# Attention probabilities turned by VectorE in 32x32 squares and a round trip through DRAM, in place of TensorE transposes

## The chip, the cores and the metric

One core of one Trainium2 chip runs the whole program in a single launch. The metric is the device time of one execution in microseconds (us). Of the kernel before, three runs gave a median of 2538.5 us.

## What is computed

A trunk of two layers works on one sequence of 1024 tokens with 1024 features in f32. Layer 0 mixes tokens with a gated MLP and a gated delta rule; layer 1 with differential attention; both have an MLP and a gated projection behind the mixing. The change touches only the attention of layer 1, whose core is:

```python
for each of 8 heads, each block of 128 queries:
    logits = einsum('qrd,krd->rqk', q_blk, k) - slope * dist      # r = 0, 1: two maps, 64 features each
    logits = where(dist >= 0, logits, -inf)
    probs = softmax(logits, axis=-1)
    attn = probs[0] - lam * probs[1]                              # (128 queries, keys)
    o = einsum('qk,ke->qe', attn, v)                              # e = 128 value features
o = rms_norm(o, sub_gain) * (1 - lam_init)
```

The product with the values sums over keys. TensorE sums over the partition, so `attn`, which is made with queries on the partitions, has to be turned to have keys there.

## The kernel before

**Work of the stage.** `attention` (L872) runs 64 blocks, eight for each of eight heads; block b of a head has 128 queries and the n = 128(b+1) keys up to its own. A block makes its two maps of logits on TensorE (`logits`, L1002); VectorE takes them out of PSUM with the position term and keeps a running minimum (L1016); ScalarE takes the exponential with the sum (L1019). `combine` (L1021) forms map 0 plus a factor times map 1 on VectorE, over n columns, in place in map 0. `transpose` (L1029) turns each 128x128 square on TensorE into a PSUM tile `pt` of four squares (L1035), and ScalarE copies that to an SBUF tile `aT` (L1037). `value` (L1039) multiplies by the values, one product for each block of keys (L1046), and takes the result out (L1047, L1049); after each fourth block o is scaled on GpSimd and stored (L1065). Map 0 has three buffers that take turns (`lg0`), map 1 has one (`lg1`), and `aT` three (`aT_tag`, L953).

**Work between.** While a head attends, the projections of the heads to come run in between: q and k of the next head, and half of a set of values for two heads (`proj_qk`, `proj_v`, L908 and L932), 24 units for a head. Their weights come by SP's queue into eight raw buffers (L101), are split into a high part on ScalarE (L223) and a low part on GpSimd (L224), and each unit is 12 products of 256 columns. In the last head there are no projections left; parts of the output projection take their place, which load and store h (`mix_part`, L1165).

**Order.** The main loop (L1133) is written as a pipeline. In turn g it emits: logits of map 0 of block g, `combine` of block g-1, a share of the projections, `transpose` of block g-2, a share, logits of map 1 of block g, a share, `value` of block g-2, a share. This is a priority and not the final order: when the program is built, a planner lays out each engine's instructions by estimated times, so that later work may be put ahead of earlier work that isn't ready. On the chip each engine then takes its own list strictly in order, SP's list of transfers too.

**Values.** A tile of values (`A0`, `A1`) holds two heads' 256 features for all tokens, tile t of 128 tokens with one token on each partition. ScalarE writes it from PSUM in L938, and the products of L1046 read it.

Of the kernel before, what the change touches and what calls it, by code (L numbers as in the profile page):

```python
# [11 lines left out]
F32 = mybir.dt.float32  # L12
F32R = mybir.dt.float32r
AF = mybir.ActivationFunctionType
ALU = mybir.AluOpType
# [3 lines left out]
P = 128  # L19
# [3 lines left out]
NT = S // P  # L23
HT = 512
# [90 lines left out]
class Trunk:  # L115
# [731 lines left out]
    def attn_consts(self, q_gain, k_gain, lam, sub_gain, lam_init):  # L847
# [21 lines left out]
        nc.vector.tensor_scalar(nl, nl, -lam_init, None, ALU.add)  # L869
        self.qg, self.kg, self.sg, self.nlam = qg, kg, sg, nl  # L870

    def attention(self, w_qkv, w_out, gain_next, h_dram):  # L872

        nc = self.nc
        NB = NT
        hs, r = list(self.hs), list(self.r)
# [16 lines left out]
        def proj(label, srcs, t2s, evac):  # L893
            def units(w):
                for t2 in t2s:
                    ps = self.mm_ps()
                    for i in range(2):
                        h, c = tok(2 * t2 + i)
                        for k in range(KT):
                            self.mm3(ps[:, 256 * i : 256 * (i + 1)], [x[:, c] for x in hs[h][k]], w.at(k), k == 0, k == KT - 1)  # L900
                            if k == 3 or (k == 7 and i == 0):
                                yield None
                    yield evac(t2, ps)

            n = 256 // len(srcs)
            return Proj(label, [(ap, i * n) for i, ap in enumerate(srcs)], 256, units, 4 * len(t2s), nc.gpsimd)

        def proj_qk(hd, qk):  # L908
# [20 lines left out]

            return proj(f"qk{hd}", [w_qkv[:, i * D + hd * P : i * D + (hd + 1) * P] for i in range(2)], range(4), evac)  # L930

        def proj_v(pr, hf, out):  # L932
            def evac(t2, ps):
                if len(out) == pr:
                    out.append(self.slot(f"A{pr % 2}", [P, NT, 256], F32, "v"))
                for i in range(2):
                    t = 2 * t2 + i
                    nc.scalar.activation(out[pr][:, t, :], ps[:, 256 * i : 256 * (i + 1)], AF.Copy, scale=r[t // 4][:, t % 4 : t % 4 + 1])  # L938

            return proj(f"v{pr}", [w_qkv[:, 2 * D + pr * 256 : 2 * D + (pr + 1) * 256]], (2 * hf, 2 * hf + 1), evac)  # L940

# [8 lines left out]
        lg0 = [lgs[0][:, 0], lgs[0][:, 1], lgs[1][:, 0]]  # L950
        lg1 = lgs[1][:, 1]
        qk_tag = itertools.cycle(("aux", "sc", "aux"))
        aT_tag = itertools.cycle(("c8", "c9", "c10"))  # L953
        heads = {}

        def begin(hd):

            qk = qks[hd]

            ks = self.slot(f"A{2 + hd % 2}", [P, 2, S], F32R, "ks")  # L960

            def put_k(hf):
                pt = self.aux([P, HT], "tr", "tr")
                for t in range(4):
                    self.pe.transpose(pt[:, t * P : (t + 1) * P], qk[1][hf][:, t, :], self.ident)
                for r in range(2):
                    own, other = half[r], half[1 - r]
                    dst = ks[:, r, hf * HT : (hf + 1) * HT]
                    nc.scalar.activation(dst[own], pt[own], AF.Copy, scale=self.kg[own])
                    nc.vector.scalar_tensor_tensor(dst[other], pt[own], self.kg[own], f32(dst[own]), ALU.mult, ALU.subtract)  # L970

            def put_q(b2):
                pt = self.aux([P, HT], "tr", "tr")
                for i in range(2):
                    self.pe.transpose(pt[:, i * P : (i + 1) * P], qk[0][b2 // 2][:, 2 * (b2 % 2) + i, :], self.ident)
                qh = self.slot(f"c{11 + b2 % 2}", [P, 2, 2 * P], F32R, "qh")
                ql = qlow[b2 % 2]
                for r in range(2):
                    own, other = half[r], half[1 - r]
                    nc.scalar.activation(qh[own, r], pt[own, 0 : 2 * P], AF.Copy, scale=self.qg[own])  # L980
                    nc.vector.tensor_copy(qh[other, r], f32(qh[own, r]))
                    nc.vector.scalar_tensor_tensor(ql[own, r], pt[own, 0 : 2 * P], self.qg[own], f32(qh[own, r]), ALU.mult, ALU.subtract)
                return qh, ql

            put_k(0)
            heads[hd] = [ks, put_k, put_q, put_q(0)]

        class Block:
# [32 lines left out]
            def combine(me):  # L1021
                b, n, sums = me.b, me.n, me.sums

                rs = self.sp.tile([P, 1], F32, tag="rs", name=self.nm("rs"))
                nc.vector.reciprocal(rs, sums[:, b, 1:2])
                nc.vector.scalar_tensor_tensor(rs, sums[:, b, 0:1], self.nlam, rs, ALU.mult, ALU.mult)
                nc.vector.scalar_tensor_tensor(me.lg[0][:, :n], me.lg[1][:, :n], rs, me.lg[0][:, :n], ALU.mult, ALU.add)

            def transpose(me):  # L1029
                me.aT = []  # L1030
                for c in range((me.n + HT - 1) // HT):
                    k0, k1 = 4 * c, min(me.b + 1, 4 * c + 4)
                    pt = self.aux([P, HT], "tr", "tr")
                    for k in range(k0, k1):
                        self.pe.transpose(pt[:, (k - k0) * P : (k - k0 + 1) * P], me.lg[0][:, k * P : (k + 1) * P], self.ident)  # L1035
                    me.aT.append(self.slot(next(aT_tag), [P, HT], F32, "aT"))
                    nc.scalar.copy(me.aT[c][:, : (k1 - k0) * P], pt[:, : (k1 - k0) * P])  # L1037

            def value(me):  # L1039
                hd, b = me.hd, me.b  # L1040
# [53 lines left out]
        qks, vs, os = [[] for _ in range(8)], [], [[] for _ in range(8)]  # L1094

        projs = [proj_v(0, 0, vs), proj_qk(0, qks[0]), proj_v(0, 1, vs)]
        for hd in range(1, 8):
            projs.append(proj_qk(hd, qks[hd]))
            if hd < 7:
                projs.append(proj_v((hd + 1) // 2, (hd + 1) % 2, vs))  # L1100
# [8 lines left out]
        def pump():  # L1109
            i = state[0] = state[0] + 1  # L1110
            for (i0, u0), (i1, u1) in zip(marks, marks[1:]):
                if i0 < i <= i1:
                    want = u0 + (u1 - u0) * (i - i0) / (i1 - i0)
                    while state[1] < want:
                        next(fill)
                        state[1] += 1
            if i > TAIL:
                next(tail, None)
# [13 lines left out]
        blocks = []  # L1132
        for g in range(8 * NB + 2):  # L1133
            if g < 8 * NB:
                hd, b = divmod(g, NB)
                blocks.append(Block(hd, b))
                blocks[g].logits(0)
            if 0 < g <= 8 * NB:
                blocks[g - 1].combine()
            pump()  # L1140
            if g < 8 * NB and b % 2 and b < NB - 1:
                q = heads[hd][2]((b + 1) // 2)
            if g > 1:
                blocks[g - 2].transpose()
            pump()
            if g < 8 * NB:
                if b == 3 - (hd < 7):
                    heads[hd][1](1)
                blocks[g].logits(1)
            pump()  # L1150
            if g > 1:
                blocks[g - 2].value()
            pump()
            if g < 8 * NB:
                if b % 2 and b < NB - 1:
                    heads[hd][3] = q
                if b == 6 + (hd == 6) and hd < 7:
                    begin(hd + 1)
# [824 lines left out]
```

## Time and profile before

| | |
|---|---|
| median of three runs | 2538.5 us (2537.97 to 2539.23) |
| the profiled execution: its span, first to last instruction | 2535.2 us |
| median less span | 3.3 us |
| TensorE, matmul records | 2515.3 us, 99% of the span |
| VectorE | 1854.3 us, 73% |
| ScalarE | 1285.9 us, 51% |
| GpSimd | 285.5 us, 11% |
| DMA of the core | 396.92 MB in 298,818 packets, mean 157 GB/s |

The profile gives no time of the profiled execution other than its span, from the first to the last instruction. PE is TensorE's multiplication, PEld its loading of weights, which runs beside it; DVE is VectorE, ACT ScalarE, POOL GpSimd, SP the engine that issues the transfers. A busy time is the union of an engine's records. Durations of single matmuls overlap, since they are pipelined, so the spacing of a row of them says more than the length of one. The granted TensorE clock was full nearly throughout (mean 0.999).

### The profile page before, as it was taken

The numbers are of one execution on the slowest core, as the hardware profiler recorded it, in microseconds if no ns is written. First come the engines' busy times: TensorE is split into PE (matmuls) and PEld (weight loads), VectorE is DVE, ScalarE is ACT, GpSimd is POOL, SyncE is SP. The second block draws the span as 40 slices with busy tenths as digits, with TensorE's granted clock in tenths as the row PEclk, the third lists the DMA queues.
The fourth block names the chain that finished last, engine by engine and source line by source line (L and its number), as shares of the span: only waits on it lengthen the run. The fifth ranks groups of instructions, "written<-read, shape, count | busy, mean of one in ns | idle before, by whom it ended". The sixth has DMA issues, their size and how long they took to land.

```text
span 2535.2 us, 40147 instructions
## 1 busy us (share of the span) xinstructions
PE 2515.3 (99%) x14046; PEld 2151.9 (85%) x14046; DVE 1854.3 (73%) x3676; ACT 1285.9 (51%) x2553; POOL 285.5 (11%) x256
## 2 busy tenths in 40 slices
PE   9999999999999999999999999999999999999999
PEld 7898898888888878888999999988778888888877
DVE  7867776697666888656477777787887677787586
ACT  6543444465455434544366666665654555445452
POOL 0301232000000000000334333310000000000000
PEclk9999999999999999999999999999999999999999
DMA  7452435457557756553211111147466558655651
GB/s 242 126 157 78 136 110 193 138 175 242 161 174 257 245 164 207 183 158 120 74 53 47 55 47 43 59 136 257 143 219 202 174 184 281 216 184 185 200 178 59
DMA packets 298818, 396.92 MB, mean 157 GB/s; under 512 B 37780, under 2 KB 165752, under 8 KB 298616
## 3 DMA queue, kind: packets, MB, share of 16 engines
q1 hardware_dynamic: 298600, 394.36, 48.4%
q8 instruction: 110, 1.80, 0.3%
q14 instruction: 92, 0.75, 0.1%
q10 hardware_dynamic: 16, 0.00, 0.0%
HBM read 289.40 MB, written 104.86 MB: 156 GB/s over the span
## 4 chain that ended last, share of the span: by engine, by line
PE 92%; DVE 4%; DMA 2%; issue 1%; ACT 1%; SPq 0%; POOL 0%; DVEq 0%; ACTq 0%; POOLq 0%
PE mm L76 79%; PE po L76 3%; PE qk L76 2%; PE aux L76 2%; PE tr L79 2%; DMA raw<-in_w_ple_gate_dram 1%; DVE lg L1016 0%; DVE w L224 0%; DMA raw<-in_w_mlp_dram 0%; PE pz L76 0%; PE py L76 0%; PE aux L79 0%; PE pvn L76 0%; PE pab L79 0%; PE pkq L76 0%
## 5 line engine op out<-in xcount | busy, mean ns | idle before, releaser
L76 PE MATMUL mm<-g,w 128*128 128x512 f32 x2592 | 603.6, 394 | 0.8 <-DVE g L224 0.5
L223 ACT CAST w<-raw 128x512 fp32r<-128x512 f32 x598 | 366.0, 618 | 453.8 <-PE mm L76 386.8
L76 PEld LDWEIGHTS mm<-g,w 128*128 128x128 f32 x2592 | 485.9, 188 | 116.2 <-DVE g L224 1.0
L76 PE MATMUL mm<-hi,w 128*128 128x512 f32 x1728 | 553.6, 396 | 0.3 <-ACT hi L1219 0.3
L76 PE MATMUL mm<-w,hi 128*128 128x256 f32 (+2 forms) x2528 | 505.5, 295 | 0.0
L224 DVE TENSOR_TENSOR w<-raw,w 128x512 fp32r<-128x512 f32 x534 | 364.8, 690 | 178.9 <-ACT w L223 169.4
L76 PEld LDWEIGHTS mm<-w,hi 128*128 128x128 f32 x2528 | 400.1, 188 | 13.6 <-DVE acc L284 0.3
L76 PEld LDWEIGHTS mm<-hi,w 128*128 128x128 f32 x1728 | 324.7, 188 | 73.7 <-ACT hi L1219 0.7
L76 PE MATMUL mm<-w,lo 128*128 128x256 f32 (+2 forms) x1264 | 370.3, 293 | 0.0
L76 PE MATMUL mm<-lo,w 128*128 128x512 f32 x864 | 341.6, 396 | 0.9 <-DVE lo L1220 0.9
L76 PE MATMUL mm<-t,w 128*128 128x512 f32 x1152 | 270.9, 394 | 1.2 <-ACT w L223 1.2
L76 PEld LDWEIGHTS mm<-t,w 128*128 128x128 f32 x1152 | 216.2, 188 | 52.8 <-ACT w L223 1.6
L76 PEld LDWEIGHTS mm<-w,lo 128*128 128x128 f32 x1264 | 238.2, 188 | 5.6
L76 PEld LDWEIGHTS mm<-lo,w 128*128 128x128 f32 x864 | 162.8, 188 | 36.8 <-DVE lo L1220 1.4
L224 DVE TENSOR_TENSOR g<-graw,g 128x512 fp32r<-128x512 f32 x216 | 147.2, 685 | 8.8 <-DMA gd<-g 6.9
L223 ACT CAST g<-graw 128x512 fp32r<-128x512 f32 x216 | 132.7, 617 | 32.8 <-issue 10.9
L1019 ACT ACTIVATE lg<-lg,nm 128x128 f32<-128x128 f32 (+7 forms) x128 | 99.5, 777 | 82.5 <-DVE nm L1016 76.0
L260 POOL TENSOR_TENSOR r<-ms,mhalf 128x4 f32<-128x4 f32 x12 | 13.3, 1109 | 1060.9 <-DVE ms L258 1033.5
L350 ACT ACTIVATE g<-g 128x512 f32<-128x512 f32 x96 | 60.6, 632 | 114.8 <-DVE g L284 114.5
L1016 DVE CUSTOM_DVE_ANT_0 lg<-qk,al 128x512 f32<-128x512 f32 (+3 forms) x128 | 75.1, 589 | 36.2 <-PE qk L76 32.8
L224 POOL TENSOR_TENSOR w<-raw,w 128x512 fp32r<-128x512 f32 x64 | 84.6, 1347 | 111.9 <-ACT w L223 63.0
L76 PE MATMUL mm<-ohi,w 128*128 128x512 f32 x256 | 85.2, 400 | 0.5 <-ACT ohi L1073 0.5
(336 smaller groups left out, 3612.4 us busy)
## 6 DMA issues: line engine op xcount, KB each, us to landing
raw<-in_w_mlp_dram SPq DMA_DIRECT2D x352, 256.0 KB, 3.3
graw<-gd SPq DMA_DIRECT2D x224, 256.0 KB, 2.8
gd<-g SPq DMA_DIRECT2D x192, 256.0 KB, 3.1
raw<-in_w_ple_gate_dram SPq DMA_DIRECT2D x76, 256.0 KB, 3.5
acc<-h_dram SPq DMA_DIRECT2D x64, 256.0 KB, 4.4
keep<-in_w_mlp_dram SPq DMA_DIRECT2D x64, 256.0 KB, 4.3
raw<-in_w_in_e_dram SPq DMA_DIRECT2D x60, 256.0 KB, 3.7
h_dram<-acc SPq DMA_DIRECT2D x48, 256.0 KB, 2.5
```

The lines of the kernel that those rows point to most:

```text
L76: self._next(self.engine.matmul(*a, **k))
L79: self._next(self.engine.transpose(*a, **k))
L223: self.nc.scalar.copy(hi, src)
L224: (lo_engine or self.nc.vector).tensor_tensor(lo, src, f32(hi), ALU.subtract)
L260: nc.gpsimd.tensor_tensor(r, ms, self.mhalf[:, 0:4], ALU.pow)
L350: nc.scalar.activation(g, src, AF.Relu)
L1016: nc.vector.tensor_tensor_reduce(out=lg[:, k0:k1], in0=ps[:, : k1 - k0], in1=al[:, u0 + k0 : u0 + k1], scale=-1.0, scalar=3.0e38 if c == 0 ...
L1019: nc.scalar.activation(lg[:, :n], lg[:, :n], AF.Exp, bias=nm[:, r, nch - 1 : nch], scale=-1.0, accum_out=me.sums[:, b, r : r + 1])
```

## The change

The turning of `attn` leaves TensorE and ScalarE. `combine` writes into map 1's buffer, and VectorE turns every 32x32 square of it in place of the square, into map 0's buffer. What then lies in partition 32i+c, column 32j+r of a block of keys is query 32i+r and key 32j+c. One transfer stores the block's rows to a new DRAM tile in pieces of 512 B; one transfer for each four blocks of keys loads them back in pieces of 128 B, so that partition 4c+j holds key 32j+c, and its columns are the 128 queries in order. That is a complete turn, but for the order of keys in the partitions. The sum over keys doesn't depend on the order if the values have the same: so each half set of values is stored from its tile by four transfers (32 partitions each) and loaded back into the same place with token 32j+r of a tile on partition 4r+j.

`transpose` of a block is now emitted right behind its `combine`, one turn of the loop earlier than before, and `aT` gets a fourth buffer (`attn_tile`), in a place that holds a sum of squares outside this stage.

```diff
+    def attn_tile(self, tag):
+        if tag.startswith("c"):
+            return self.slot(tag, [P, HT], F32, "aT")
+        return self.sp.tile([P, HT], F32, tag=tag, name=self.nm("aT"), bufs=1)
...
+        v_drams = [self.dp.tile([NT, 32, 4, 256], F32, name=self.nm("v_dram")) for _ in range(4)]
...
+                if t2 % 2:
+                    ts = slice(4 * hf, 4 * hf + 4)
+                    for j in range(4):
+                        nc.sync.dma_start(v_dram[ts, :, j].rearrange("t r f -> r t f"), out[pr][32 * j : 32 * j + 32, ts])
+                    nc.sync.dma_start(out[pr][:, ts], v_dram[ts].rearrange("t r j f -> (r j) t f"))
...
-        aT_tag = itertools.cycle(("c8", "c9", "c10"))
+        aT_tag = itertools.cycle(("c8", "c9", "c10", "sqs0"))
...
-                nc.vector.scalar_tensor_tensor(me.lg[0][:, :n], me.lg[1][:, :n], rs, me.lg[0][:, :n], ALU.mult, ALU.add)
+                nc.vector.scalar_tensor_tensor(me.lg[1][:, :n], me.lg[1][:, :n], rs, me.lg[0][:, :n], ALU.mult, ALU.add)
 
             def transpose(me):
+
+                n, nk = me.n, me.b + 1
+                nc.vector.transpose(me.lg[0][:, :n], me.lg[1][:, :n])
+                a_dram = self.dp.tile([nk, P, P], F32, name=self.nm("a_dram"))
+                nc.sync.dma_start(a_dram.rearrange("k p c -> p k c"), me.lg[0][:, :n].rearrange("p (k c) -> p k c", c=P))
+                src = a_dram.rearrange("k (i r) (j c) -> k (r j) i c", r=32, c=32)
                 me.aT = []
-                for c in range((me.n + HT - 1) // HT):
-                    k0, k1 = 4 * c, min(me.b + 1, 4 * c + 4)
-                    pt = self.aux([P, HT], "tr", "tr")
-                    for k in range(k0, k1):
-                        self.pe.transpose(pt[:, (k - k0) * P : (k - k0 + 1) * P], me.lg[0][:, k * P : (k + 1) * P], self.ident)
-                    me.aT.append(self.slot(next(aT_tag), [P, HT], F32, "aT"))
-                    nc.scalar.copy(me.aT[c][:, : (k1 - k0) * P], pt[:, : (k1 - k0) * P])
+                for k0 in range(0, nk, 4):
+                    k1 = min(nk, k0 + 4)
+                    aT = self.attn_tile(next(aT_tag))
+                    nc.sync.dma_start(aT[:, : (k1 - k0) * P].rearrange("p (k i c) -> p k i c", i=4, c=32), src[k0:k1].rearrange("k p i c -> p k i c"))
+                    me.aT.append(aT)
...
                 blocks[g - 1].combine()
+                blocks[g - 1].transpose()
             pump()
...
-            if g > 1:
-                blocks[g - 2].transpose()
```

More of the change, by code (lines that the diff above doesn't have):

```diff
@@ L935, in evac @@
                     out.append(self.slot(f"A{pr % 2}", [P, NT, 256], F32, "v"))
+                v_dram = v_drams[pr]
                 for i in range(2):
```

## The prediction

> **What bounds the kernel now.** I read the page first: its busy line and the chain that ended last.
>
> ```profile
> span 2535.2 us, 40147 instructions
> PE 2515.3 (99%) x14046; PEld 2151.9 (85%) x14046; DVE 1854.3 (73%) x3676; ACT 1285.9 (51%) x2553; POOL 285.5 (11%) x256
> PE 92%; DVE 4%; DMA 2%; issue 1%; ACT 1%; SPq 0%; POOL 0%; DVEq 0%; ACTq 0%; POOLq 0%
> ```
>
> TensorE is the chain. To a first approximation, work taken off it is time, and work put on another engine is free until that engine or its latency comes last. The change touches only the attention stage. The tiles that it touches say where that is: the turned probabilities start at 1278.6 us, and the last product with the values at 1742.9 (an f32 product is two records, so 576 are 288 products; the third row, from the groups of the stage, is the copy that takes the turned squares out of PSUM).
>
> ```profile
> L79 PEld LDWEIGHTS tr<-ident,lg x288: 137/141/147, 1278.6 to 1737.6; 128*128 128x128 f32 x144
> L76 PE MATMUL po<-v,aT x576: 270/275/377, 1282.9 to 1742.9; 128*128 128x128 f32 x192
> ...
> L1037 ACT COPY aT<-tr 128x512 f32<-128x512 f32 (+2 forms) x96 | 44.7, 476 | 16.8 <-PE tr L79 16.1
> ```
>
> Then the stage by windows. Between the combines of block 7 in two successive heads (below, at 1380.93 and 1439.10) lie 58.2 us, one head. I cut it in thirds, and add the last head. The columns are busy times of PE, PEld, DVE, ACT and POOL, then the granted clock, the DMA share and GB/s.
>
> ```profile
> 1380.90:1400.00 19.10, 19.10 (x163) 19.01 (x164) 10.30 (x32) 13.04 (x37) 6.57 (x7) 1.00 0.20 57
> 1400.00:1420.00 20.00, 20.00 (x161) 19.43 (x161) 16.00 (x50) 10.22 (x27) 4.44 (x3) 1.00 0.04 14
> 1420.00:1439.10 19.10, 18.13 (x141) 17.31 (x140) 17.15 (x45) 12.39 (x27) 11.34 (x9) 1.00 0.23 70
> sum 58.20, PE 57.23 PEld 55.74 DVE 43.45 ACT 35.64 POOL 22.36; mean PE 19.08 PEld 18.58 DVE 14.48 ACT 11.88 POOL 7.45
> 1676.00:1734.00 58.00, 57.32 (x326) 48.58 (x325) 46.71 (x119) 34.07 (x80) 5.72 (x6) 1.00 0.47 152
> ```
>
> TensorE is full in every third. VectorE is not second by a wide margin everywhere: half idle in the first third, 2 us short of full in the last one, where the long rows of keys are. That is the number to keep in mind, because the change moves work onto it.
>
> **TensorE and ScalarE: what goes.** 288 transposes leave TensorE. Their records overlap, so the duration of one (141 ns for the weights) is too much; I take the spacing where six follow each other:
>
> ```profile
> 1484.54 0.46 PEld L79 LDWEIGHTS tr<-ident,k 128*128 128x128 f32 x4
> 1484.96 0.25 PEld L79 LDWEIGHTS tr<-ident,q 128*128 128x128 f32 x2
> 1485.18 0.19 PEld L76 LDWEIGHTS qk<-ks,qh 128*128 128x128 f32 x1
> ```
>
> Six take 1485.18 - 1484.54 = 0.64 us, 0.107 each. 288 x 0.107 = 30.8 us, 3.85 a head (36 each), and a full TensorE gives all of it back if nothing else comes last: **-30.8 us**. ScalarE loses its 96 copies, 44.7 us or 5.6 a head; it is 61% busy (35.64 of 58.2), so that is worth nothing by itself.
>
> **VectorE: what comes.** One transpose over the n columns of each of the 64 blocks. The trace has this instruction elsewhere, at one size; the combine gives the slope of an instruction that streams one column after the other.
>
> ```profile
> L1644 DVE STREAM_TRANSPOSE inv<-inv x8: 300/311/314, 190.5 to 368.1; 128x128 f32<-128x128 f32 x8
> L1027 DVE SCALAR_TENSOR_TENSOR lg<-lg,rs,lg 128x1024 f32<-128x1024 f32 x6 | 7.7, 1285 | 0.2
> L1027 DVE SCALAR_TENSOR_TENSOR lg<-lg,rs,lg 128x640 f32<-128x640 f32 x6 | 5.3, 880 | 0.1
> L1027 DVE SCALAR_TENSOR_TENSOR lg<-lg,rs,lg 128x128 f32<-128x128 f32 x5 | 1.8, 352 | 0.2
> ```
>
> (1285 - 352) / 896 = 1.04 ns a column. With that slope a transpose is 311 - 133 = 178 ns + 1.04 n: 1.24 us for 1024 columns, and per head 8 x 0.178 + 4608 x 0.00104 = 6.2 us. If its whole 311 ns grew with the columns (2.43 ns each), it would be 11.2. I take 6.2, as a fixed part near 0.2 us is what the combine shows too (352 - 133 = 219). The Trainium skill ("VectorE: DVE Perf Modes", The three transpose paths) gives 311 ns for a 128x128 VectorE transpose in bf16 and 390 for TensorE's, and its rules for authors send a 128x128 transpose to TensorE; the row above agrees on the 311, for f32 too, and in this full TensorE stream its transpose costs 107. By the page's 390 the gain would be an estimated 112 us.
>
> By thirds, transposes of blocks 7, 0 and 1 fall into the first (1.24 + 0.31 + 0.44 = 2.0), of 2 to 4 into the second (2.1), of 5 and 6 into the last (2.1). TensorE needs a third of its 3.85 less in each. First third: 12.3 us of VectorE in 17.8 of TensorE, hidden. Second: 16.0 + 2.1 = 18.1 in 18.7. Last: 17.15 + 2.1 = 19.3 against 17.8, not hidden. VectorE also can't be full: its idle time (4.0 and 1.95 us in these two) is waiting for logits and exponentials that are made in the same stretch. If it keeps half of that, these thirds take 20.1 and 20.2. Sum 17.8 + 20.1 + 20.2 = 58.1, against 58.2: VectorE hands back **+30** of the 30.8. Bounds: all idle time is filled and TensorE sets 54.3 (nothing handed back); it keeps all 14.75 us of it (58.2 - 43.45 + 43.45 + 6.2 = 64.4, 50 us slower than before over 8 heads). The half is a choice between these, as the order of all queues is laid out anew at build time and can't be read here. Behind a transpose in VectorE's queue stand the minima and evacuations of the next logits, and TensorE waits for those through their PSUM tiles: that is how the time is handed back.
>
> **The round trip.** 36,864 packets of 512 B go out and 147,456 of 128 B come back (288 blocks of keys x 128 and x 512). Two windows show what packets cost: one with only the small ones of L1640 and a few of 2 KB, one of the stage itself.
>
> ```profile
> DMA packets 904, 0.14 MB, mean 23 GB/s; under 512 B 864, under 2 KB 904, under 8 KB 904
> q1 hardware_dynamic: 904, 0.14, 12.4%
> inv<-solved SPq DMA_DIRECT2D x6, 16.0 KB, 1.7
> ...
> q1 hardware_dynamic: 3552, 2.62, 14.8%
> raw<-in_w_qkv_o_dram SPq DMA_DIRECT2D x8, 128.0 KB, 2.3
> ...
> guv<-uv_dram SPq DMA_DIRECT2D x5, 512.0 KB, 5.5
> ```
>
> 260 to 266 us: 0.124 x 6 us x 16 / 904 = 13 ns for 155 B on average. 1440 to 1500: 0.148 x 60 x 16 / 3552 = 40 ns for 738 B. On the line between them 128 B cost 12 ns and 512 B 30. So a head adds 18,432 x 12 / 16 + 4,608 x 30 / 16 = 13.8 + 8.6 = 22 us to each DMA engine, beside some 9 now (15%): rate is no bound, with the dearer 40 ns for each as the bad end. The Trainium skill ("DMA: Bandwidth & Descriptors", Specifications) speaks against this change: 512 B is its least transfer for line rate, and below that it tells of a read-modify-write. The rows agree in bytes (155 / 13 = 12 B a ns against 738 / 40 = 18), but not in packets: a small one is the cheaper.
>
> Latency: landing of a small transfer is 1.7 us. A store of block 7 has 64 packets an engine, 1.7 + 1.9 = 3.6 us; a load of four blocks of keys 128, 1.7 + 1.5 = 3.2. From the start of the combine: 1.28 + 1.24 + 3.6 + 3.2 = 9.4 us with hand-offs left out; block 4: 0.88 + 0.84 + 2.9 + 3.2 = 7.8, and 0.4 for its second tile. The product that needs it comes now:
>
> ```profile
> 1380.93 1.28 DVE L1027 SCALAR_TENSOR_TENSOR lg<-lg,rs,lg 128x1024 f32<-128x1024 f32 x1
> 1391.72 1.06 PE L76 MATMUL po<-v,aT 128*128 128x128 f32 x8
> 1415.72 0.87 DVE L1027 SCALAR_TENSOR_TENSOR lg<-lg,rs 128x640 f32<-128x640 f32 x1
> 1425.05 1.28 PE L76 MATMUL po<-v,aT 128*128 128x128 f32 x10
> 1439.10 1.28 DVE L1027 SCALAR_TENSOR_TENSOR lg<-lg,rs 128x1024 f32<-128x1024 f32 x1
> ...
> SPq L101 <- POOL w L224: 177.0, 48, 25.7
> 1373.44 21.80 SPq L101 DMA_DIRECT2D raw<-in_w_qkv_o_dram  x10
> ```
>
> 10.8 us after the combine for block 7, 9.3 for block 4: about 1 us to spare in both, and these are the two tightest. But both transfers go through SP's queue, in order with the weight loads (L101), each of which waits for POOL. Around block 7 ten of these follow each other in 21.8 us, one in 2.2; a store and a load that each meet half such a wait come 2.2 us later, so block 7 is late by about 1 us in each of the seven heads that have this burst: **+7 us**, bounds 0 and 3 us a head (24). The load waits in SP's queue for its store to land (3.6 us); behind it stand weight loads, for ScalarE's casts and eight buffers ahead, and the stores of o (L1065), read only in the last head: these have tens of us. Buffers: three logits tiles and, now, four for the turned ones, each free an iteration before it is taken again; the fourth uses space that no square sum needs in this stage.
>
> **Values.** Eight half sets of values get four stores and one load each behind ScalarE's writing, some 2.3 + 5.5 = 8 us by the landings of 128 and 512 KB above. A first half is written a head ahead of its use, a second about three of eight blocks into a head whose block 4 first needs it, one to two blocks, 7 us and more, later: nothing, and a single wait of a few us if that cover were gone. **The last head** has a DMA share of 0.47 and 11 us of VectorE idle of 58; 22 us more of DMA makes it 0.85, while its own loads of h feed VectorE: I put **+3 us** (0 to 12) beside no gain there.
>
> Sum: -30.8 + 30 + 7 + 3 = +9 on the span of 2535.2, so 2544. The runs' median of 2538.5 lies 3.3 above that span; **2547 us**.
>
> **Rivals.**
> - *VectorE's idle time takes the transposes, faster.* For it: ScalarE sheds 5.6 us a head, so exponentials come sooner, and the projections can be moved into VectorE's slack first third. Against: the last third. If VectorE keeps only a sixth of its idle time in the two late thirds, they take some 18.8 and 19.6, a head 56.2: -16, so 2522 with no block late. With the 10 us of the late blocks and the last head in place it decides below a head of 56.3, without them below 57.6 (5 us past them over 8 heads).
> - *Packets of 128 B cost 40 ns like the mean one of the stage.* A head then needs (18,432 + 4,608) x 40 / 16 = 58 us of DMA beside 9 and values' 3, 70 instead of 58: +94, 2632. Against it: the 13 ns above; it decides from 32 ns, where 70 falls to 58. The 512 B rule of the Trainium skill (same page and section) would bring this about.
> - *2.43 ns a column on VectorE:* 43.45 + 11.2 + half of its idle 14.75 = 62 us a head, +31, and 10 as in the forecast: 2579.
>
> **Chances.** This measurement can tell 0.2%, 5 us, from no change. Forecast (slower, its own range 2544 to 2565) 0.36; faster rival 0.37; its edge, within 5 us of 2538.5, 0.13; dear packets 0.08, dear transposes 0.06. Slower together 0.50. The range from 2512 (between the fast rival and TensorE's bound of 2538.5 - 31 = 2507) to 2600 (dear transposes, and late blocks at 24) leaves out the dear packets and a little at the fast end.
>
> **What would show it.** Transposes of lg off TensorE and its busy time there down by 30 us or its idle time up; STREAM_TRANSPOSE near 1.24 us at 1024 columns; VectorE over 90% busy in the stage; a wait of PE's for aT's DMA, mostly for block 7; DMA share from 0.15 to about 0.55. Wrong: PE still full and a head at 55 us; DMA share at 0.9; waits for aT in every block.

## The result, and the profile after

The changed kernel takes 2550.1 us, the median of four runs (2548.4 to 2554.0), against 2538.2 for the kernel before: a ratio of 1.005 [1.0036, 1.0065], slower by 12 us. 2547 was predicted. The sum is right to 3 us, but two of its parts, VectorE's and the round trip's, are wrong by over 20 us each, in opposite directions. The experiments below are about these two.

The profiled execution (2548.4 us) has a span of 2546.7 us, 11.5 over that of before. Its busy lines, its first queue and its chain, from the page of the kernel after:

```profile
span 2546.7 us, 39945 instructions
PE 2497.1 (98%) x13758; PEld 2126.6 (84%) x13758; DVE 1900.0 (75%) x3740; ACT 1243.5 (49%) x2457; POOL 286.9 (11%) x256
...
q1 hardware_dynamic: 494312, 440.51, 57.1%
...
PE 86%; DVE 5%; DMA 5%; issue 1%; ACT 1%; SPq 1%; POOL 0%; DVEq 0%; ACTq 0%; POOLq 0%
```

288 matmul instructions are gone and TensorE's records are busy for 18 us less, yet the span is longer: TensorE now stands idle for some 50 us, where it was 20. In the chain TensorE falls from 92% to 86%, and DMA rises from 2% to 5%.

The stage by windows, cut at the combines of block 7: first the six heads 1 to 6, then the last head, then from the last combine to the last product with the values. Before:

```profile
1321.50:1664.00 342.50, 339.86 (x2745) 331.51 (x2744) 256.55 (x753) 213.50 (x531) 123.06 (x103) 1.00 0.17 52
1664.00:1726.80 62.80, 61.48 (x350) 52.02 (x349) 51.25 (x137) 38.02 (x90) 6.35 (x7) 1.00 0.44 145
1726.80:1743.00 16.20, 15.73 (x99) 13.54 (x97) 7.86 (x13) 6.57 (x15) 0.00 (x0) 1.00 0.63 201
```

After:

```profile
1326.50:1665.80 339.30, 323.54 (x2522) 310.24 (x2522) 293.95 (x805) 183.81 (x458) 125.11 (x102) 0.99 0.68 158
1665.80:1734.70 68.90, 61.67 (x331) 50.37 (x330) 55.86 (x146) 33.70 (x81) 5.11 (x6) 1.00 0.79 202
1734.70:1755.10 20.40, 16.78 (x84) 13.93 (x83) 8.47 (x13) 3.21 (x7) 0.00 (x0) 0.92 0.98 280
```

- The first window starts 5 us later (1326.5 against 1321.5): +5.0. In it TensorE waits 3.0 us for turned probabilities of head 0.
- The six heads: 339.3 against 342.5, so -3.2. TensorE's transposes alone would make that 6 x -3.85 = -23. TensorE's idle time (window less busy) grew from 2.6 to 15.8 us; VectorE went from 256.6 to 294.0 us, 87% busy; the DMA share from 0.17 to 0.68.
- The last head +6.1, the last trip to the last product +4.2, everything behind it -0.6, which adds up to the 11.5.

What TensorE waited for in the stage (1260 to 1780 us; total, times, longest), before:

```profile
PE po L76 <- ACT aT L1037: 0.4, 2, 0.2
```

And after, with VectorE's wait that stands behind the second row:

```profile
PE po L76 <- DMA aT<-a_dram: 13.5, 13, 2.6
PE mm L76 <- DVE t L1194: 13.0, 5, 4.9
...
DVE t L1194 <- DMA t<-h_dram: 12.2, 7, 2.9
```

Two waits are new. The product waits for the turned probabilities, 13.5 us. The output projection waits for VectorE's sum `t`, which waits for a load of h, 13.0 us; that is at the end of the stage.

**Which blocks come late.** TensorE's timeline at three of the waits (a block b has 2(b+1) records, so x4 is block 1 and x6 block 2):

```profile
1297.49 0.91 PE L76 MATMUL po<-v,aT 128*128 128x128 f32 x6 [2.60 <-DMA aT<-a_dram]
...
1406.34 0.68 PE L76 MATMUL po<-v,aT 128*128 128x128 f32 x4 [1.49 <-DMA aT<-a_dram]
...
1465.23 0.68 PE L76 MATMUL po<-v,aT 128*128 128x128 f32 x4 [1.45 <-DMA aT<-a_dram]
```

Nine of the thirteen waits, 10.1 of the 13.5 us, are at blocks 0 to 2, the short ones at the beginning of a head; none is at block 7. (The other four are at block 6, twice, and at blocks 4 and 5 of the last head.) SP's queue ahead of the wait at 1406.34 shows how such a block comes late. First VectorE, which has turned block 1 by 1394.2, then SP (the L1047 are stores, the L1053 loads):

```profile
1393.78 0.45 DVE L1045 STREAM_TRANSPOSE lg<-lg 128x256 f32<-128x256 f32 x1
```

```profile
1387.28 0.36 SPq L1047 DMA_DIRECT2D a_dram<-lg  x1
1390.53 1.67 SPq L1053 DMA_DIRECT2D aT<-a_dram  x2
1392.29 1.29 SPq L1047 DMA_DIRECT2D a_dram<-lg  x1
...
1395.20 1.38 SPq L950 DMA_DIRECT2D v_dram<-v  x3
1396.69 0.39 SPq L1053 DMA_DIRECT2D aT<-a_dram  x1
1397.12 0.55 SPq L950 DMA_DIRECT2D v_dram<-v  x1
1397.77 0.38 SPq L1047 DMA_DIRECT2D a_dram<-lg  x1
1398.20 1.53 SPq L101 DMA_DIRECT2D raw<-in_w_qkv_o_dram  x3
1399.83 0.41 SPq L951 DMA_DIRECT2D v<-v_dram  x1
1400.33 0.46 SPq L1053 DMA_DIRECT2D aT<-a_dram  x1
```

1387.28 is block 7's store, 1390.53 its two loads, behind the landing of the store. Block 0's store (1392.29) stands behind these, its load (1396.69) behind that store's landing, 4.4 us for 64 KB. Only then comes block 1's store (1397.77), 3.5 us after its transpose ended, and its load at 1400.33; the product starts at 1406.34. So a trip waits for its own two landings and for every trip ahead of it in a queue that keeps its order. Over all heads, the 32 stores of blocks 4 to 7 go out within 0.04 us of their transposes; of the 24 stores of blocks 0 to 2 only nine do so within 1 us, and the others are 1.1 to 3.6 us late. The landings (KB, median us from issue), from the list of DMA issues:

```profile
aT<-a_dram SPq DMA_DIRECT2D x48, 256.0 KB, 3.7
...
a_dram<-lg SPq DMA_DIRECT2D x8, 512.0 KB, 3.2
...
a_dram<-lg SPq DMA_DIRECT2D x8, 192.0 KB, 4.9
...
a_dram<-lg SPq DMA_DIRECT2D x8, 64.0 KB, 4.6
```

A store of 64 KB takes longer to land than one of 512 KB. It goes out just behind block 7's loads of 4,096 short packets; where these loads come in pieces of 512 B (a run below), the stores of 64 KB land in 2.0 us.

### The profile page after: what moved, and what is told of

It reads as the page before. It is cut to its first block, busy times and chain, and to the rows that moved or that the text cites. A ratio compares the mean times of both kernels' runs of the same rounds, so it can differ in the third digit from the quotient of the medians.

```text
span 2546.7 us, 39945 instructions
## 1 busy us (share of the span) xinstructions
PE 2497.1 (98%) x13758; PEld 2126.6 (84%) x13758; DVE 1900.0 (75%) x3740; ACT 1243.5 (49%) x2457; POOL 286.9 (11%) x256
## 3 DMA queue, kind: packets, MB, share of 16 engines
q1 hardware_dynamic: 494312, 440.51, 57.1%
## 4 chain that ended last, share of the span: by engine, by line
PE 86%; DVE 5%; DMA 5%; issue 1%; ACT 1%; SPq 1%; POOL 0%; DVEq 0%; ACTq 0%; POOLq 0%
PE mm L76 76%; PE aux L76 2%; PE po L76 2%; DMA aT<-a_dram 2%; PE qk L76 2%; DMA t<-h_dram 1%; DVE lg L1029 1%; PE tr L79 1%; DVE lg L1040 1%; DMA a_dram<-lg 1%; DVE lg L1045 1%; DMA raw<-in_w_mlp_dram 1%; DVE w L224 0%; DMA h_dram<-t 0%; DVE ql L995 0%
## 5 line engine op out<-in xcount | busy, mean ns | idle before, releaser
L76 PEld LDWEIGHTS mm<-w,hi 128*128 128x128 f32 x2528 | 401.2, 188 | 15.8 <-issue 1.3
L260 POOL TENSOR_TENSOR r<-ms,mhalf 128x4 f32<-128x4 f32 x12 | 13.3, 1108 | 1060.1 <-DVE ms L258 1031.8
L76 PE MATMUL po<-v,aT 128*128 128x128 f32 x576 | 80.0, 281 | 15.3 <-DMA aT<-a_dram 13.5
```

Source lines behind the costliest of these rows:

```text
L76: self._next(self.engine.matmul(*a, **k))
L260: nc.gpsimd.tensor_tensor(r, ms, self.mhalf[:, 0:4], ALU.pow)
```

## The experiments

Two theories run through the expectations. **V** is the prediction's: VectorE, nearly full, hands back what TensorE gives. **T**: the trip through DRAM is what costs it, and VectorE's idle time takes the transposes. T has parts of its own, told apart later: the number of packets, the traffic as such, or the time from a block's combine to its product. Where not stated otherwise, short diffs are against the changed kernel, and ratios against the kernel before in the same call (2537.1, 2537.5, 2538.5 and 2537.8 us in the four).

**VectorE's transposes alone.** The kernel before, with one line behind the combine:

```diff
+                nc.vector.transpose(me.lg[1][:, :n], me.lg[0][:, :n])
```

> The kernel before, with VectorE's transpose of each block added behind its combine; its result goes into the free buffer of map 1 and is not used, and TensorE still turns the squares. So VectorE's +50 us stand alone. Theory V (VectorE's queue is what hands TensorE's saving back, as predicted): the two later thirds of a head get about 20.1 and 20.2 us instead of 20.0 and 19.1, +1.2 us a head, about 2548. Theory T (the round trip is late at the product with the values, and VectorE has room): within 3 us of before, 2536 to 2541, VectorE's busy time up by 50.

2544.9 us, 1.0032 [1.0019, 1.0045]. Its six heads by windows:

```profile
1325.28:1676.41 351.13, 343.61 (x2747) 333.19 (x2746) 295.16 (x803) 211.30 (x534) 123.96 (x103) 1.00 0.17 52
```

58.5 us a head against 57.1: with TensorE still full, 6.2 us more of VectorE cost 1.4 of a head (rather less in the median: this profile is of a run 3 us above it). Added work is mostly, not wholly, hidden. That is near V's number for this run, but under a quarter of the 6.2 us, and it doesn't say what is left when TensorE is lighter.

**The change without the trip.** VectorE turns the squares, and the product takes them as they are; values stay in their own order:

```diff
-                a_dram = self.dp.tile([nk, P, P], F32, name=self.nm("a_dram"))
...
+                me.aT = [me.lg[0][:, k0 * P : min(nk, k0 + 4) * P] for k0 in range(0, nk, 4)]
```

> The changed kernel without any round trip: VectorE still turns the 32x32 squares, and the product with the values takes them straight from that buffer; the values stay in their own order. It leaves out the moving of squares between partitions, so the output is another one; TensorE's and VectorE's work is that of the changed kernel. Theory V: no gain over before, 2535 to 2540, a head near 58. Theory T: TensorE's saving comes through, 2538 - 31 + a few for VectorE = 2508 to 2518, heads of 54.5 to 56.

2511.9 us, 0.9902 [0.9887, 0.9916]. Its six heads:

```profile
1322.88:1647.97 325.09, 318.77 (x2516) 307.46 (x2515) 293.03 (x803) 182.29 (x457) 123.35 (x102) 1.00 0.19 57
```

This decides between the two. With all of VectorE's added work in place a head takes 54.2 us, against 57.1 before, and VectorE is 90% busy: 2.9 of the 3.85 us a head come through. Of the 30.8 us that TensorE gives, 25 arrive in the whole time. V falls. The trip, all of it, costs 2550.1 - 2511.9 = 38 us.

The two profiled spans, 37.3 us apart, tell where it is paid: 3.6 us ahead of block 7 of head 0, 14.2 in the six heads, and 19.5, the larger half, in the last head and behind it. In the six heads TensorE idles 9.5 us more than without the trip (15.8 against 6.3), and its waits there for turned probabilities add up to 9.4.

**Is it the number of packets?** The load comes back in runs of 512 B, a quarter of the packets:

```diff
-                    nc.sync.dma_start(aT[:, : (k1 - k0) * P].rearrange("p (k i c) -> p k i c", i=4, c=32), src[k0:k1].rearrange("k p i c -> p k i c"))
+                    nc.sync.dma_start(aT[:, : (k1 - k0) * P].rearrange("p (k i c) -> p k i c", i=4, c=32), a_dram[k0:k1].rearrange("k p (i c) -> p k i c", c=32))
```

> The changed kernel, but the load back takes whole rows of 512 B in place of pieces of 128 B: the same bytes, waits and order of queues, a quarter of the packets on the way back; keys come back in the wrong partitions, so the output is another one. If the number of packets matters (the DMA engines at 0.68 of their time in the six middle heads and 0.98 behind the last): that share falls to about 0.5, loads land in under 3 us instead of 3.7, and the time is 2535 to 2543. If only the chain of two landings matters: 2545 to 2550. Theory V: as the changed kernel, 2549 to 2551.

2546.9 us, 1.0041 [1.0026, 1.0056], overlapping the changed kernel's 1.0036 to 1.0065. 110,592 packets fewer, the DMA share of the six heads at 0.54 in place of 0.68, and the loads land sooner, but the time is nearly the same:

```profile
q1 hardware_dynamic: 383720, 440.51, 54.6%
...
aT<-a_dram SPq DMA_DIRECT2D x48, 256.0 KB, 3.0
```

The product still waits 14.0 us for the load. The number of packets is not the main cause: it is worth 3 us of the 38, which this measurement doesn't tell from none. The trace shows one thing more. Now 19 of the 24 stores of blocks 0 to 2 go out within 1 us of their transposes, and yet the waits stay, since TensorE comes sooner too: its product for block 2 starts 9.5 us after the combine in place of 12.1 (medians of seven heads).

**Without the values' trip.**

```diff
-                if t2 % 2:
...
-                    nc.sync.dma_start(out[pr][:, ts], v_dram[ts].rearrange("t r j f -> (r j) t f"))
```

> The changed kernel without the stores and loads of the values, which stay in their own order, so the products pair the wrong keys and the output is another one. Every theory so far, and the prediction, takes these 40 transfers to be hidden: 2547 to 2551. If they stand in the way of the probabilities in SP's queue or on the DMA engines in the middle heads: 3 to 8 us less.

2546.4 us, 1.0032 [1.0018, 1.0047]; the wait at the product is 12.0 us. Some 4 us under the changed kernel and just under the expected range, but the two intervals overlap, so it can't be told from none. The cost is mainly the probabilities' trip.

**A turn more for the trip.** Nothing moved but the product: it takes block g-3 instead of g-2, and two more buffers (six) hold the turned blocks meanwhile.

```diff
-        aT_tag = itertools.cycle(("c8", "c9", "c10", "sqs0"))
+        aT_tag = itertools.cycle(("c8", "c9", "c10", "sqs0", "sqs1", "rb1"))
...
-        for g in range(8 * NB + 2):
+        for g in range(8 * NB + 3):
...
-            if g > 1:
-                blocks[g - 2].value()
+            if g > 2:
+                blocks[g - 3].value()
```

> The changed kernel with the product with the values emitted one turn later (three turns behind its logits, not two) and six buffers for the turned probabilities in place of four; all work and all transfers as in the changed kernel. Theory T (the trip is too long for the 1.75 turns that it has): TensorE no longer waits for it in the first seven heads, where it costs about 25 us, the end of the last head stays as it is: 2523 to 2533. If the trip costs by traffic on SP's queue or the DMA engines instead: 2545 to 2552. Theory V: 2545 to 2552.

2527.7 us, 0.9963 [0.9948, 0.9978], 22 us under the changed kernel, and now faster than the kernel before. Its wait at the product, and its six heads:

```profile
PE po L76 <- DMA aT<-a_dram: 2.3, 4, 1.1
```

```profile
1326.08:1652.85 326.77, 318.95 (x2507) 307.18 (x2506) 293.02 (x807) 184.98 (x461) 124.89 (x102) 1.00 0.71 165
```

The same transfers, the same packets, a DMA share of 0.71, and the six heads take 326.8 us, 1.7 from those with no trip at all. So traffic and packets cost the middle of the stage next to nothing; the time between combine and product was short, and that was the cost there. By the median of seven heads, the product of a block started 10 to 12 us after its combine in the changed kernel, and starts 11 to 16 us after it here (block 2: 12.1 and 16.3).

The two buffers changed along with the product, but a lack of them is not what held the trip: in the changed kernel, wherever the trace has the landing of a store, its load goes out within 0.8 us of it. And not all of the 22 us are the middle's. Of the 19.2 us between the two profiled spans, 12.5 are in the six heads and 6.3 in the last head and behind it, where the wait for `t` falls from 13.0 to 3.1 us. The expectation had left that end as it was.

**The last two heads turned by TensorE.** Heads 6 and 7 keep the old way (TensorE's transposes, ScalarE's copies, values in order); the product is where the change has it.

```diff
-                if t2 % 2:
+                if t2 % 2 and pr < 3:
...
-                blocks[g - 1].transpose()
+                if blocks[g - 1].hd < 6:
+                    blocks[g - 1].transpose()
...
+            if g > 1 and blocks[g - 2].hd >= 6:
+                blocks[g - 2].turn()
```

> The changed kernel with heads 6 and 7 turned by TensorE and ScalarE as before, and their values left in their own order; heads 0 to 5 as changed. The last head has no projections to fill TensorE, and its trips share SP's queue and the DMA engines with the loads of h. If that is where about 12 us of the loss arise (the last head 6 us longer, its last trip 4, a lower clock behind it 1 to 3): 2536 to 2541. If the loss is spread over all heads alike: 2543 to 2548. Theory V: near 2549.

2534.9 us, 0.9989 [0.9979, 0.9998]: 15 us under the changed kernel, a little better than expected. The wait at the product stays, as it should (13.3 us, ten times); the end of the stage is mended. Four windows show it, first of the kernel after, then of this one:

```profile
1740.00:1760.00 20.00, 13.36 (x59) 10.46 (x57) 6.71 (x13) 4.19 (x11) 2.65 (x3) 0.91 0.98 284
1760.00:1780.00 20.00, 18.11 (x71) 14.70 (x72) 10.74 (x17) 6.11 (x10) 0.00 (x0) 0.83 0.80 267
```

```profile
1740.00:1760.00 20.00, 20.00 (x105) 16.74 (x104) 11.18 (x21) 7.84 (x15) 2.25 (x3) 1.00 0.79 269
1760.00:1780.00 20.00, 20.00 (x88) 16.18 (x87) 17.32 (x29) 10.77 (x19) 0.00 (x0) 1.00 1.04 371
```

TensorE is full there again, and the granted clock with it. In the kernel after, the means of 0.91 and 0.83 are short falls to half: the clock records of its trace show 0.50 for 3.4 us from 1746.4 and for 6.8 us from 1760.0, about the ends of waits of 3.6 and 4.9 us, and 1.00 between and behind them. The Trainium skill ("TensorE: Matmul & The Clock Gate", Part 1) has the clock at half after an idle window of about 3.4 us; the trace agrees on the half and on the step of 3.4 us. It doesn't agree that it takes an idle time of that length: at 1330.0 the clock falls for 3.4 us about the end of a wait of 1.8 us, while waits of 2.6 and 2.7 us (ending at 1297.5 and 1733.6) bring no fall.

**Both edits together**, on two chips.

> Both edits: heads 0 to 5 by the trip with the product one turn later, heads 6 and 7 by TensorE. Theory T with the separate end: TensorE's saving of six heads, 6 x 3.85 = 23 us, less some 5: 2517 to 2524, faster than both kernels. If the trip costs by traffic: 2535 to 2541.

2517.4 us, 0.9924 [0.9907, 0.9941]. The same kernel again:

> Heads 0 to 5 by the trip with the product one turn later, heads 6 and 7 by TensorE, once more, for its profile at full clock: 2515 to 2520; TensorE waits for the trip's load less than 3 us in all.

2520.9 us, 0.9929 [0.9914, 0.9944], some 0.9 over its range. Waits at the product, and its six heads:

```profile
PE po L76 <- DMA aT<-a_dram: 1.1, 1, 1.1
```

```profile
1324.43:1646.44 322.01, 316.94 (x2511) 306.37 (x2510) 285.23 (x790) 184.43 (x461) 124.71 (x102) 1.00 0.63 147
```

Together the two edits bring 29 to 33 us, somewhat less than 22 + 15, as the later product alone had already eased the end. What is left to the kernel without a trip is 5 to 9 us, of which two heads' transposes, 2 x 3.85, are kept on TensorE by the edit itself.

**The store in halves.** Transpose and store are cut at four blocks of keys, so that the first half leaves earlier:

```diff
+                for k0 in range(0, nk, 4):
+                    cs = slice(k0 * P, min(nk, k0 + 4) * P)
+                    nc.vector.transpose(me.lg[0][:, cs], me.lg[1][:, cs])
+                    nc.sync.dma_start(a_dram[k0 : min(nk, k0 + 4)].rearrange("k p c -> p k c"), me.lg[0][:, cs].rearrange("p (k c) -> p k c", c=P))
```

> The changed kernel with transpose and store of a block cut in two at four blocks of keys, so that the first load can start when the first half has landed: for blocks 4 to 7 the first tile comes 1 to 2 us sooner, for one more transfer each and 0.2 us more of VectorE. Theory T: blocks 4 and 7 are the tight ones, so 1 to 2 us in most heads, 2538 to 2547. If SP's queue is what costs (32 transfers more): 2550 to 2556. Theory V: 2550 to 2552.

2543.2 us, 1.0025 [1.0015, 1.0035], some 7 us under the changed kernel, but not where it was expected. The wait at the product is not shorter (16.4 us in 15 waits), and neither are the six heads (340.4 us). The profile, which shows 2.6 us of the gain, has 6.2 us less in the last head and behind it and 3.6 more ahead of that. So a trip cut in halves is not shown to help the middle, and the later product does much more.

**Only the last head by TensorE**, with the later product, in the hope of keeping one head's gain more (of the last values only head 6's half is reordered).

> Heads 0 to 6 by the trip with the product one turn later, head 7 alone by TensorE; of the last set of values only head 6's half is reordered. Theory T with the separate end: as with heads 6 and 7 by TensorE (2517), less head 6's 3.85 us of transposes: 2511 to 2517. If head 6's trips, too, collide with the loads and stores of the output projection, which begins in it: 2517 to 2524.

2520.7 us, 0.9931 [0.9915, 0.9948], the same as with two heads. That is the rival's number. Its reason is not shown: the product waits 4.6 us, but only 1.0 of these at a block of head 6. From block 7 to block 7, head 6 takes 57.7 us against 52.9 with TensorE's transposes, and the last head 57.5 against 62.1, so work has moved between the two; where the 3.85 us of head 6's transposes are spent stays open.

**The same with the copies of o on ScalarE**, to see whether VectorE's queue holds what is left.

```diff
-                nc.vector.tensor_copy(o[b // 4][:, b % 4, :], po)
+                nc.scalar.copy(o[b // 4][:, b % 4, :], po)
```

> Heads 0 to 6 by the trip with the product one turn later, head 7 by TensorE, and the 64 copies of o out of PSUM on ScalarE in place of VectorE (0.29 us each, 2.3 us a head). If what is left of the loss is VectorE's queue: 3 to 8 us less than without the move, 2506 to 2512. If not: within 2 us of it.

2519.5 us, 0.9924 [0.9909, 0.9939], within 2 us of the run before. Taking 2.3 us a head out of VectorE's queue gains nothing that can be told.

**Loads from another queue.** To part SP's order from the length of the trip, the loads alone are issued by GpSimd, in the changed kernel:

```diff
-                    nc.sync.dma_start(aT[:, : (k1 - k0) * P]...
+                    nc.gpsimd.dma_start(aT[:, : (k1 - k0) * P]...
```

> The changed kernel with the loads of the turned probabilities issued from GpSimd's queue in place of SP's, so that SP no longer waits for a store to land before it issues the next block's store (111 us of such waits in the changed kernel). If SP's order is what makes the small blocks behind block 7 late: the stores of blocks 0 to 2 go out within 1 us of their transposes and the time falls to 2535 to 2544. If the length of the trip itself is what counts: 2546 to 2552. GpSimd's queue now waits for the landings, in front of its low parts of the weights: where that comes last instead, over 2552, with waits of TensorE for weights.

2588.0 us, 1.0198 [1.0181, 1.0215]: slower by 38 us more. From its page, the queue and the issuing instruction; from its waits, the product:

```profile
q0 software_dynamic: 6144, 18.88, 3.3%
```

```profile
L1053 POOL DMA_DIRECT2D aT<-a_dram x96 | 101.3, 1056 | 157.6 <-DMA a_dram<-lg 88.5
```

```profile
PE po L76 <- DMA aT<-a_dram: 26.4, 18, 5.2
```

The first half of the sign came: 20 of the 24 stores of blocks 0 to 2 now go out within 1 us of their transposes, against nine. But GpSimd spends 1.06 us on each issue and waits in order itself, and the loads of 256 KB land in 5.2 us instead of 3.7, so the probabilities come later and not sooner. The time is that of the third case, without its sign: TensorE's long waits are for the probabilities, not for weights. This edit changed more than the order, and doesn't tell the two apart. Whether a second in-order queue with SP's prices would save what the later product saves stays open.

## Why the prediction was right, and where it was wrong

**Right: sign and sum.** +9 was predicted on the span; +11.5 came. That is the rest of two larger errors that cancel, so the agreement is luck. (The 3.3 us from span to median were too much as well: the profiled run of the kernel after took 1.7 us over its span.) By terms:

- **TensorE -30.8: right.** 288 products are gone, and with no trip TensorE's busy time in the six heads falls by 339.9 - 318.8 = 21.1 us, 3.5 a head where 3.85 were worked out; 25 us arrive in the whole time. The head of 58.2 us, and with it the bound of 54.3, was one head; the mean of six was 57.1, which makes the bound 53.2, and 54.2 is 1 us above that.
- **A transpose's price: right.** The groups of the kernel after:

```profile
L1045 DVE STREAM_TRANSPOSE lg<-lg 128x1024 f32<-128x1024 f32 x8 | 9.9, 1234 | 0.0
...
L1045 DVE STREAM_TRANSPOSE lg<-lg 128x128 f32<-128x128 f32 x8 | 2.5, 309 | 0.2
```

  1.234 us at 1024 columns, against 178 + 1.04 x 1024 = 1.24; the eight sizes sum to 49.5 us, 6.2 a head. The dear case of 2.43 ns a column is out.
- **VectorE hands back +30: wrong, some 6.** The step was "if it keeps half of that": the idle time of 14.75 us a head was read as waiting that stays. The forecast's head of 58.1 us leaves VectorE 58.1 - 43.45 - 6.2 = 8.5 us idle; without the trip it idles (325.1 - 293.0) / 6 = 5.3 us a head. The head was also summed from thirds, each with its own limit, while the kernel's order is laid out anew and work can move between the thirds; how much that makes isn't measured. The rival "VectorE's idle time takes the transposes" was right about this engine: it put the head 2.0 us shorter, and it gets 2.9 shorter.
- **Round trip +7, last head +3: wrong, 38 together,** of which about 18 us come before the last head and 19.5 from it on. Two steps failed. *Place:* the trip was costed for block 7 and block 4 each alone, "these two are the two tightest", with the other blocks left at ease. Late are mainly blocks 0 to 2, whose own trips are short but queue behind block 7's. The time that a trip may take was read off the kernel before, too, and it shrank: by the medians of seven heads the product of block 1 started 19.4 us after its combine there, and 11.4 in the changed kernel. The weight loads, which were to cause the delay, lost theirs: SP's wait for GpSimd's weights fell from 177.0 to 39.2 us.

```profile
SPq L1053 <- DMA a_dram<-lg: 111.5, 50, 5.3
SPq L1047 <- DVE lg L1045: 46.9, 20, 6.8
SPq L101 <- POOL w L224: 39.2, 21, 16.9
```

  What holds SP's queue now is the trip's own two waits, 111.5 us at loads for their stores and 46.9 us at stores for their transposes. *Price:* a late load was put at 1 us a head; a turn more for it took 2.1 us off each of the six heads, and 22 us off the whole.
- **The last head** was to lose 3 us. With what follows it lost 10 against before, and 19.5 against the kernel without a trip. There are no projections left to fill TensorE there. The last trip, by the three timelines of SP, VectorE and TensorE:

```profile
1737.80 0.37 SPq L1047 DMA_DIRECT2D a_dram<-lg  x1
...
1744.12 2.74 SPq L1053 DMA_DIRECT2D aT<-a_dram  x2
```

```profile
1745.74 1.38 DVE L1194 TENSOR_TENSOR t<-t,mm 128x512 f32<-128x512 f32 x2 [2.08 <-DMA t<-h_dram]
```

```profile
1746.48 0.79 PE L76 MATMUL mm<-ohi,w 128*128 128x512 f32 x1 [3.62 <-DVE t L1194]
...
1753.41 1.95 PE L76 MATMUL po<-v,aT 128*128 128x128 f32 x16
```

  The load is issued 6.3 us after the store, and the product comes 9.3 us after that, with a DMA share of 0.98. Meanwhile the output projection waits for loads of h that share the engines. That collision was named, but priced on the mean of the head; it is paid in the last 35 us, and with a clock of 0.50 for 10 us of them, which the prediction hadn't thought of.
- **Values nothing:** 4 us at the measured medians, not told apart from none.
- **DMA no bound:** right for six heads, where the share is 0.68 (0.55 was worked out), and 0.71 with the later product costs next to nothing. (0.68 x 339.3 - 0.17 x 342.5) x 16 / 144,000 packets (six heads of 23,040, and the values' 1,000 a head) is an estimated 19 ns each, where the prediction's two prices average 16. The Trainium skill's 512 B for line rate ("DMA: Bandwidth & Descriptors", Specifications) didn't decide here: 512 B runs brought the loads from 3.7 to 3.0 us and the time down by 3 us, not told apart from none.

Shown: that VectorE's part is small (the kernel without the trip), that time between combine and product is the cost in the middle (the later product, the same traffic), and that the end is a cost of its own (the last two heads). Argued only: that it is SP's order, rather than the two landings by themselves, that sets the waits. The queue's timeline shows the short blocks' stores held up, but in two runs most of these stores go out at once and the product waits no less: with loads in 512 B pieces, where the product comes sooner as well, and with loads from GpSimd, which land later.

## What to carry to other kernels

Here a hop through DRAM cost two landings and the transfers ahead of it in SP's queue, so follow the queue from block to block, above all the small blocks behind the large one, rather than cost each trip alone; and give the hop another turn of the loop (two buffers here) before judging it: the same work and transfers went from 12 us slower than before to 10 us faster. Keep the old way where the loop runs out of other work: the last two heads alone were worth 15 us, and both edits together make the best whole kernel here, 0.993 of the time before. When a prediction rests on how much idle time an engine keeps, try the added work without the added latency first; here that one run moved 24 us from one term to another.

## What was not expected of the hardware

- VectorE ran 90% busy over 325 us with TensorE at 98%: its idle time shrank from 14.3 to 5.3 us a head when work was put into it.
- A store of 64 KB landed in 4.6 us where one of 512 KB took 3.2, when it ran behind loads of 128 B packets; behind the same loads in 512 B packets it landed in 2.0.
- The granted clock fell to 0.50 for 3.4 or 6.8 us at a time about the ends of TensorE's waits of 1.8, 3.6 and 4.9 us, on a single busy core, and not at waits of 2.6 and 2.7 us.
- The same loads issued by GpSimd went as 6,144 packets of 3 KB instead of 147,456 of 128 B, and still landed later, at 1.06 us of GpSimd for each issue.
